# Half of one adaLN vector computed on another engine, and three changes of order, in a two-layer diffusion trunk

## The chip, the cores and the metric

The kernel runs on one core of one Trainium2 chip. The metric is the device time of one execution in microseconds. Five engines work side by side, each on its own in-order queue: PE (TensorE) multiplies matrices, DVE (VectorE) and ACT (ScalarE) work elementwise, POOL (GpSimd) does very little here, and SP (SyncE) issues nearly all DMAs.

## The reference, cut to what matters

All arrays are float32: 256 latent tokens and 256 context tokens of width 2048, two layers. Layer 0 mixes tokens with a bidirectional RG-LRU block, layer 1 with a multi-scale pooling mixer; each is followed by a SwiGLU feed-forward network (FFN) of hidden width 5632. Every sub-layer is wrapped by adaLN and a DeepNorm post-norm:

```
m = split(silu(c) @ mod_w[i] + mod_b[i], 6)           # six vectors of 2048 per layer
h = x * (1 + m[1]) + m[0]
x = LN(ALPHA * x + m[2] * mixer(h)) * ln_g[i,0] + ln_b[i,0]
h = x * (1 + m[4]) + m[3]
x = LN(ALPHA * x + m[5] * ((silu(h @ w1) * (h @ w3)) @ w2)) * ln_g[i,1] + ln_b[i,1]
```

Each adaLN vector is a product of one row of 2048 with a 2048 x 2048 matrix of 16 MB. The change concerns `m[4]` of layer 0, written (0, 4) below: the scale of the first FFN's input.

## The kernel before, in words

**Products.** A float32 product is made of three TensorE products: each operand is cut into a high part (`hi`, a rounded copy, by ACT, line 205) and a low part (`lo`, the rest, by DVE, line 206). `mm3` (lines 229 to 232) issues hi x hi, lo x hi and hi x lo into one PSUM bank. So each 512 KB tile of weights (`raw`, four buffers) costs one DMA, one ACT copy, one DVE subtraction and 12 to 24 matmuls.

**Stages.** The head computes the first adaLN columns (`mu_job`, eight loads of two 256 KB pieces for chunk 0) and the first 256 channels of the modulated input (`xc_job` loads context and latents, `fin_a` and `fin_b` modulate them). The front (24 to 177 us) does the other chunks and part of the RG-LRU input projection of pairs 0 to 4. The pair loop (177 to about 655 us) goes over 8 pairs of RG-LRU blocks: input projection (`wx_job`: 3 jobs in each of pairs 0 to 4, 8 in each of pairs 5 to 7, since `SPLIT` is 5), convolution, gate projection (8 `gate_job`), block gates and the recurrence, whose elementwise work runs on DVE and ACT. Then come the output projection, FFN 0, the pooling mixer with its four groups (about 1560 to 1615 us), FFN 1 and the last normalization.

**adaLN vectors in the loop.** Besides its own work the loop computes three adaLN vectors in two ways. `mod_chunk` works on PE: for 512 columns it loads eight pieces of 512 KB, multiplies them with the conditioning vector (`cm`, line 367, four products side by side in four strips of 32 rows), copies the bank out (`keep_part`) and turns the row into columns with four small matmuls (line 387). Vector (0, 4) is made of four such chunks. `mod_jobs` works on DVE: for 1024 columns it loads sixteen 512 KB tiles (`mraw`, two buffers) and adds each, times one conditioning scalar, to an accumulator (`acc`, two buffers; line 267, the first of the sixteen on line 264 or 261). `sums` then adds over the partitions with two matmuls per 512 columns (lines 302 and 303), and `finish_cols` copies the row to DRAM and reads it back as columns (lines 308 to 320). Vectors (0, 3) and (0, 2) go this way, 64 tiles in all; (0, 2) has no `sums` there, since `row_now` (line 335) makes it after the loop.

**Order.** A list of jobs `J` is written out by hand; `spread_mod` lays a lane of jobs (the adaLN work) among the jobs of the loop by a density per job. `Runner` goes through the list: loads are issued ahead as far as the buffers of their class allow, the hi/lo cuts up to three weight jobs ahead of the products. A job that is a `barrier` holds back the cuts of all later jobs until it has been reached. At build time a planner then fixes each engine's queue: among the instructions that are ready by its own estimates it takes the earliest in this order, and inside `tc.high_priority(HP)` an instruction counts as 400 places earlier. So work whose data are ready can move far ahead of its place.

**The pool's end.** For each pool group g, `pool_job(g, 1)` first restores the affine of the earlier norm on its 512 columns (`restore`: times `rowg`, plus `rowb`, lines 863 and 864, for two halves of the tokens), then finishes the products, adds them to the residual (`residual`, lines 836, 839 and 842, the last being the statistics) and, for g = 3, makes the moments (lines 852 to 854). `pool_end` reloads `rowg` and `rowb` by DMA; then FFN 1 begins with `hidden_t` (lines 949 to 969): normalize, transpose on PE, modulate and cut. `hidden_t`, and `residual` for g = 3, run at high priority.

Of the kernel before, what the change touches and what calls it, by code (L numbers as in the profile page):

```python
# [10 lines left out]
F32 = mybir.dt.float32  # L11
F32R = mybir.dt.float32r
AF = mybir.ActivationFunctionType
ALU = mybir.AluOpType
# [4 lines left out]
KT = D // 128  # L19
# [3 lines left out]
PAIRS = 8  # L23
PW = 352
SPLIT = 5
ROWS = (128, 128, 96)
WINDOWS = (2, 4, 8, 16)
ALPHA = 4.0 ** 0.25
# [4 lines left out]
HP = 400  # L33
# [124 lines left out]
def trunk(es, tc, x, ctxlat, cols_in, ccols, mod_w, mod_b, ln_g, ln_b, ffn_w1, ffn_w3, ffn_w2,  # L158
# [34 lines left out]
    def plain(fn):  # L193
        j = Job()
        j.use = lambda _: fn()
        return j
# [111 lines left out]
    def finish_cols(layer, which, n, bank):  # L308
# [5 lines left out]
        if n == D // MW - 1:  # L314
# [4 lines left out]
            b = cols[:, C_MODB + (layer * 6 + which) * KT:C_MODB + (layer * 6 + which + 1) * KT]  # L319
            nc.vector.tensor_tensor(t, m, b, op=ALU.add)  # L320

    def finish_row(layer, which, n, bank, width=MW):
        c = st["row", layer, which][:, n * width:(n + 1) * width]
        nc.vector.tensor_tensor(c, bank, c, op=ALU.add)
        if (n + 1) * width == D and layer == 1 and which == 2:
            pool_rows()
# [15 lines left out]
    def mod_chunk(layer, which, n):  # L342
        js = []
        ready = []
        out = {}

        def piece(q):
            j = Job()
            j.cls = "mp"

            def load():
                raw = P.tile([128, 1024], F32, name="jit", bufs=3)
                nc.sync.dma_start(raw.rearrange("p (a f) -> p a f", a=2),
                                  mod_w[layer, q * 256:(q + 1) * 256,
                                        which * D + n * 512:which * D + (n + 1) * 512]
                                  .rearrange("(a p) f -> p a f", p=128))
                return raw

            def use(j):
                ready.append((q, j.raw))  # L360
                if q % 2 == 0:
                    return
                for r, raw in ready:
                    for a in range(2):
                        kk = 2 * r + a
                        g = kk % 4
                        nc.tensor.matmul(bk[MBANK][32 * g:32 * g + 32, :], cm[:, kk, :],
                                         raw[:, a * 512:(a + 1) * 512], start=kk < 4, stop=kk >= 12)
                ready.clear()
                R.free("mp")  # L370
                R.free("mp")
                if q == 7:
                    keep_part()

            j.load = load
            j.use = use
            return j

        def keep_part():
            out[0] = P.tile([128, 512], F32, name="mh")  # L380
            nc.scalar.copy(out[0], bk[MBANK])

        def columns():
            m = out[0]
            b = bk[MBANK]
            for a in range(4):
                nc.tensor.matmul(b[:, 2 * a:2 * a + 2], m[:, a * 128:(a + 1) * 128], selt, start=True, stop=True)
            if n == 0:
                mcols[layer, which] = P.tile([128, KT], F32, name=f"mc{layer}{which}")
            o = C_MODB + (layer * 6 + which) * KT + 4 * n  # L390
            nc.vector.tensor_tensor(mcols[layer, which][:, 4 * n:4 * n + 4],
                                    b[:, 0:8].rearrange("p (a s) -> p a s", s=2)[:, :, 0],
                                    cols[:, o:o + 4], op=ALU.add)

        js = [piece(q) for q in range(8)]
        js.append(None)
        js.append(plain(columns))
        return js

# [60 lines left out]
    def xc_job(u):  # L460
        j = Job()
        j.cls = "xc"

        def load():
            xc = S_pool.tile([128, 2, 512], F32, name="xc", bufs=2)
            nc.sync.dma_start(xc, ctxlat[u * 256:(u + 1) * 256, :].rearrange("(a p) t -> p a t", p=128))
            chunks[u] = xc
            v = xc[:, :, 256:].rearrange("p a (r c) -> p a r c", r=4)
            if u < 4:
                e = per[:, 2 * u:2 * u + 2].unsqueeze(3).broadcast_to((128, 2, 4, 64))  # L470
            else:
                e = pec[:, 2 * u - 8:2 * u - 6].unsqueeze(2).broadcast_to((128, 2, 4, 64))
            nc.gpsimd.tensor_tensor(v, v, e, op=ALU.add)

        j.load = load
        j.use = lambda _: None
        return j
# [90 lines left out]
    def head():  # L568
        for q in range(8):
            J.append(mu_job(0, q))  # L570
            if q == 5:
                J.append(xc_job(0))
        J.append(plain(lambda: (fin_a(0), fin_b(0))))

    head()
# [137 lines left out]
    def recur(p, d):  # L713
# [50 lines left out]
        for f in (f2, f3, f4, f5):  # L764
# [3 lines left out]
    VF = [(0, 5, finish_row), (1, 1, finish_cols), (1, 0, finish_cols),  # L768
          (1, 3, finish_cols), (1, 4, finish_cols), (1, 2, finish_row)]
    loop = []  # L770
    for p in range(PAIRS):
        k0 = 10 if p < SPLIT else 0
        for kt in range(k0, KT, 2):
            loop.append(wx_job(p, kt, 0, kt == k0, kt == KT - 2))
        if p:
            loop.extend(gates(p - 1, 1))
        loop.append(plain(lambda p=p: conv(p)))
        for kt in range(0, KT, 2):
            loop.append(gate_job(p, kt))
        loop.extend(gates(p, 0))  # L780
    ml = []
    for n in range(4):
        ml += mod_chunk(0, 4, n)
    loop = spread_mod(loop, ml, [(len(loop), 1)])
    mv = mod_jobs([(0, 3, finish_cols), (0, 2, None)])
    loop = spread_mod(loop, mv, [(len(loop), 1)])


    def open_rows():
# [409 lines left out]
    def pool_job(g, q):  # L1199
        def use(j):  # L1200
            hi, lo = j.hl

            def token(tok):
                for a in range(2):
                    kt = 4 * g + 2 * q + a
                    ts = slice(tok * 128, (tok + 1) * 128)
                    mm3(bk[4 + (2 * g + tok) % 4], st["ph"][:, kt, ts], st["pl"][:, kt, ts],
                        hi[:, a * 512:(a + 1) * 512], lo[:, a * 512:(a + 1) * 512],
                        q == 0 and a == 0, q == 1 and a == 1)

            held.append(token)
            if q == 0 and g < PH:
                held.pop()
                token(0)
                token(1)
            if q == 1:
                for tok in range(2):
                    restore(g, tok)
                for tok in range(2):
                    for h in held:  # L1220
                        h(tok)
                    with tc.high_priority(HP if g == 3 else 0):
                        residual(bk[4 + (2 * g + tok) % 4], tok, g, st["row", 1, 2], 1.0)
                        if g == 3:
                            moments(tok)
                held.clear()
        return wjob(two_kt(pool_w[0, g], q * 256, 0, 512), 128, 1024, use)
# [11 lines left out]
    def pool_end():  # L1239
        load_ln_rows(1, 0)  # L1240
    J.append(plain(pool_end))

    f1 = ffn(1, True)
    m5 = mod_jobs([(1, 5, finish_row)])
# [106 lines left out]
```

## Time and profile before

| | us |
|---|---|
| median of three runs (2390.62 to 2395.70) | 2395.68 |
| the profiled execution | 2388.36 |
| its span | 2386.6 |
| PE busy | 2324.9 (97%) |
| DVE busy | 1758.9 (74%) |
| ACT busy | 1232.2 (52%) |
| PE idle at the pool's end, in one piece | 8.71 |

The span runs from the first to the last instruction of the profile; the execution's own time is 1.8 us longer. Busy times are unions, so a PE that is always busy may still issue more or fewer matmuls per microsecond. The granted clock of PE is full (2.4 GHz) save for a few short stretches, of which one lies at the pool's end.

### The profile page before, as it was taken

Reading aid. Unit: us, or ns where it says so; the run is one execution under the profiler, and the core shown is the slowest. Engines: PE = TensorE matmul, PEld = TensorE weight load, DVE = VectorE, ACT = ScalarE, POOL = GpSimd, SP = SyncE. Lnnn points to the kernel's source line nnn. Section 1 sums busy time; section 2 is a strip of 40 time slices with the busy share of each in tenths; the row PEclk is TensorE's granted clock in tenths of the full one; section 3 lists DMA queues with packets and bytes.
Section 4 is the critical chain, followed back from the end, with each engine's and each line's share of the span. In section 5 each row is a group of like instructions: output and inputs, shape, how many; then the busy total and the mean of one; then the engine's idle time right before and its main releaser. Section 6 shows DMA issues by size and latency. Waiting matters only on the chain. (4 is left out here: it accounts for less than half of the span.)

```text
span 2386.6 us, 29002 instructions
## 1 busy us (share of the span) xinstructions
PE 2324.9 (97%) x10488; PEld 1833.9 (77%) x10488; DVE 1758.9 (74%) x2114; ACT 1232.2 (52%) x1577; POOL 10.3 (0%) x14
## 2 busy tenths in 40 slices
PE   8999999999999999999999999998999999999997
PEld 4557777777777788877787878776878888888886
DVE  2658999887689998887887878689774544555655
ACT  3216888667685544444444455574444444444453
POOL 0000000000000000000000000000000000000000
PEclk9999999999999999999999999998999999999999
DMA  9877766776468799999999898655886656655554
GB/s 322 275 257 266 221 217 213 234 233 211 138 224 320 265 328 327 365 328 347 353 338 329 281 319 275 202 172 199 313 304 190 193 185 188 190 187 186 188 189 135
DMA packets 289704, 597.15 MB, mean 250 GB/s; under 512 B 31236, under 2 KB 99844, under 8 KB 287512
## 3 DMA queue, kind: packets, MB, share of 16 engines
q1 hardware_dynamic: 289560, 595.30, 73.9%
q8 instruction: 82, 1.34, 0.2%
q14 instruction: 62, 0.51, 0.1%
HBM read 590.20 MB, written 2.14 MB: 248 GB/s over the span
## 5 line engine op out<-in xcount | busy, mean ns | idle before, releaser
L205 ACT CAST hi<-raw 128x1024 fp32r<-128x1024 f32 (+2 forms) x740 | 733.7, 997 | 819.6 <-PE bank L231 665.9
L206 DVE TENSOR_TENSOR lo<-raw,hi 128x1024 fp32r<-128x1024 f32 (+2 forms) x740 | 849.9, 1154 | 408.8 <-ACT hi L205 390.6
L231 PE MATMUL bank<-hi,hl 128*128 128x512 f32 x1696 | 663.5, 391 | 0.0
L230 PE MATMUL bank<-hi,hh 128*128 128x512 f32 x1440 | 564.9, 393 | 0.4 <-ACT hi L205 0.3
L232 PE MATMUL bank<-lo,hh 128*128 128x512 f32 x1440 | 555.0, 392 | 5.6 <-DVE lo L206 5.0
L231 PEld LDWEIGHTS bank<-hi,hl 128*128 128x128 f32 x1696 | 319.0, 188 | 67.0 <-DVE hl L1195 0.4
L232 PE MATMUL bank<-lo,jit 128*128 128x512 f32 x880 | 347.1, 395 | 1.5 <-DVE lo L206 1.5
L230 PE MATMUL bank<-hi,jit 128*128 128x512 f32 x880 | 347.9, 396 | 0.3 <-ACT hi L205 0.3
L232 PEld LDWEIGHTS bank<-lo,hh 128*128 128x128 f32 x1440 | 270.7, 188 | 71.7 <-DVE lo L206 15.6
L230 PEld LDWEIGHTS bank<-hi,hh 128*128 128x128 f32 x1440 | 271.2, 189 | 56.7 <-ACT hi L205 1.6
L267 DVE SCALAR_TENSOR_TENSOR acc<-mraw,tiny,acc 128x1024 f32<-128x1024 f32 x172 | 220.2, 1280 | 58.2 <-DMA mraw<-in_mod_w 57.3
L232 PEld LDWEIGHTS bank<-lo,jit 128*128 128x128 f32 x880 | 165.4, 188 | 42.8 <-DVE lo L206 4.3
L230 PEld LDWEIGHTS bank<-hi,jit 128*128 128x128 f32 x880 | 165.4, 188 | 41.7 <-ACT hi L205 0.7
L231 PE MATMUL bank<-hTh,lo 128*128 128x512 f32 (+1 forms) x384 | 153.1, 400 | 0.0
L232 PE MATMUL bank<-hTl,hi 128*128 128x512 f32 (+1 forms) x384 | 151.7, 396 | 0.0
L230 PE MATMUL bank<-hTh,hi 128*128 128x512 f32 (+1 forms) x384 | 149.4, 404 | 1.8 <-ACT hTh L533 1.8
L231 PE MATMUL bank<-hi,jit 128*128 128x512 f32 x368 | 145.7, 396 | 2.6 <-DVE jit L873 2.6
L267 DVE SCALAR_TENSOR_TENSOR acc<-jit,tiny,acc 128x1024 f32<-128x1024 f32 x98 | 125.3, 1280 | 20.9 <-DMA jit<-in_mod_w 20.2
L231 PE MATMUL bank<-hi,hh 128*128 128x512 f32 x256 | 101.7, 397 | 0.0
L230 PEld LDWEIGHTS bank<-hTh,hi 128*128 128x128 f32 (+1 forms) x384 | 67.8, 179 | 40.5 <-ACT hi L205 8.4
L231 PEld LDWEIGHTS bank<-hTh,lo 128*128 128x128 f32 (+1 forms) x384 | 69.3, 181 | 28.6 <-DVE u L566 4.2
L231 PE MATMUL bank<-xh,lo 128*128 128x512 f32 (+3 forms) x224 | 89.5, 400 | 0.0
(161 smaller groups left out, 2392.2 us busy)
## 6 DMA issues: line engine op xcount, KB each, us to landing
raw<-in_ffn_w SPq DMA_DIRECT2D x528, 512.0 KB
mraw<-in_mod_w SPq DMA_DIRECT2D x184, 512.0 KB
jit<-in_mod_w SPq DMA_DIRECT2D x136, 512.0 KB
mu<-in_mod_w SPq DMA_DIRECT2D x128, 256.0 KB
raw<-in_rg_w_x SPq DMA_DIRECT2D x64, 352.0 KB
raw<-in_rg_w_gate SPq DMA_DIRECT2D x64, 352.0 KB
raw<-in_rg_w_out SPq DMA_DIRECT2D x44, 512.0 KB
raw<-in_rg_wri SPq DMA_DIRECT2D x32, 416.0 KB
```

The source lines that it names most:

```text
L205: nc.scalar.copy(hi[:k, :n], raw[:k, :n])
L206: nc.vector.tensor_tensor(lo[:k, :n], raw[:k, :n], hi[:k, :n].bitcast(F32), op=ALU.subtract)
L230: nc.tensor.matmul(bank, lh, rh, start=start, stop=False)
L231: nc.tensor.matmul(bank, ll, rh, start=False, stop=False)
L232: nc.tensor.matmul(bank, lh, rl, start=False, stop=stop)
L267: nc.vector.scalar_tensor_tensor(a, raw, c, a, op0=ALU.mult, op1=ALU.add)
```

## The change

One constant and one function are new. Vector (0, 4) is now split: columns 1024 to 2047 stay on PE (chunks 2 and 3), columns 0 to 1023 join the DVE lane, between (0, 3) and (0, 2), with the new `finish_half`. The lane's density is 0.45 over pairs 0 to 4 and 1 over pairs 5 to 7, where it was even. Counted from the lists, the lane had 34 tiles in pairs 0 to 4 and 30 in pairs 5 to 7; it now has 28 and 52. In the head, `xc_job(0)` goes behind all eight `mu_job`s, where it stood behind the sixth. `restore` for pool group 3 gets high priority. `pool_end` becomes a barrier.

```diff
+EARLY = 0.45
...
+    def finish_half(layer, which, n, bank):
+        if n == 0:
+            st["md"] = DR.tile([1, 1024], F32, name="mdh")
+        r = P.tile([128, MW], F32R, name="ml").bitcast(F32)[0:1]
+        nc.scalar.copy(r, bank[0:1, :])
+        nc.sync.dma_start(st["md"][:, n * MW:(n + 1) * MW], r)
+        if n == 1:
+            m = P.tile([128, KT], F32, name="mcr")
+            nc.sync.dma_start(m[:, :8], st["md"].rearrange("o (k p) -> p (o k)", p=128))
+            if (layer, which) not in mcols:
+                mcols[layer, which] = P.tile([128, KT], F32, name=f"mc{layer}{which}")
+            o = C_MODB + (layer * 6 + which) * KT
+            nc.vector.tensor_tensor(mcols[layer, which][:, :8], m[:, :8], cols[:, o:o + 8], op=ALU.add)
...
-            if n == 0:
+            if (layer, which) not in mcols:
                 mcols[layer, which] = P.tile([128, KT], F32, name=f"mc{layer}{which}")
...
     def head():
         for q in range(8):
             J.append(mu_job(0, q))
-            if q == 5:
-                J.append(xc_job(0))
+        J.append(xc_job(0))
         J.append(plain(lambda: (fin_a(0), fin_b(0))))
...
         for kt in range(k0, KT, 2):
             loop.append(wx_job(p, kt, 0, kt == k0, kt == KT - 2))
+            if kt == k0:
+                heads.append(loop[-1])
...
-    for n in range(4):
+    for n in (2, 3):
         ml += mod_chunk(0, 4, n)
     loop = spread_mod(loop, ml, [(len(loop), 1)])
-    mv = mod_jobs([(0, 3, finish_cols), (0, 2, None)])
-    loop = spread_mod(loop, mv, [(len(loop), 1)])
+    mv = mod_jobs([(0, 3, finish_cols), (0, 4, finish_half, 0), (0, 2, None)])
+    early = loop.index(heads[SPLIT])
+    loop = spread_mod(loop, mv, [(early, EARLY), (len(loop) - early, 1)])
...
                 for tok in range(2):
-                    restore(g, tok)
+                    with tc.high_priority(HP if g == 3 else 0):
+                        restore(g, tok)
...
     J.append(plain(pool_end))
+    J[-1].barrier = True
```

## Rows read from the trace of the kernel before

**Rows 1.** The page's first part: busy us, share of span, instructions.

```profile
PE 2324.9 (97%) x10488; PEld 1833.9 (77%) x10488; DVE 1758.9 (74%) x2114; ACT 1232.2 (52%) x1577; POOL 10.3 (0%) x14
```

**Rows 2.** Windows: stretch, length; busy PE, PEld, DVE, ACT, POOL (counts); clock, DMA, GB/s.

```profile
24.00:176.90 152.90, 152.90 (x723) 90.54 (x723) 84.09 (x165) 40.21 (x63) 7.53 (x6) 0.99 0.87 284
176.90:432.50 255.60, 253.12 (x1262) 200.86 (x1259) 237.72 (x343) 204.18 (x295) 0.00 (x0) 1.00 0.69 224
432.50:655.00 222.50, 218.05 (x1053) 170.83 (x1050) 169.55 (x231) 148.43 (x209) 0.00 (x0) 1.00 0.65 208
1632.30:2368.00 735.70, 734.47 (x3257) 601.85 (x3256) 426.79 (x416) 336.52 (x380) 0.00 (x0) 1.00 0.64 206
```

**Rows 3.** Timeline of PE around one group of `mod_chunk`, and its small matmuls.

```profile
197.93 0.32 PE L232 MATMUL bank<-lo,hTh 128*128 128x352 f32 x1
198.18 1.06 PE L367 MATMUL bank<-jit,cm 128*32 128x512 f32 x8
199.18 0.43 PE L230 MATMUL bank<-hi,hTh 128*128 128x352 f32 x1
...
294.69 0.95 PE L387 MATMUL bank<-selt,mh 128*128 128x2 f32 x8
```

**Rows 4.** Lines by form: count, busy us, mean ns, idle before.

```profile
L367 PE MATMUL bank<-jit,cm 128*32 128x512 f32 x128 | 23.9, 604 | 0.0
L302 PE MATMUL bank<-mh,onesr 128*128 128x512 f32 x32 | 12.7, 396 | 0.0
```

**Rows 5.** Tile `mraw` in 180:430 and 430:620; ns min/median/max, first and last start.

```profile
L267 DVE SCALAR_TENSOR_TENSOR acc<-mraw,tiny,acc x32: 1268/1279/1287, 182.8 to 403.4; 128x1024 f32<-128x1024 f32 x32
L267 DVE SCALAR_TENSOR_TENSOR acc<-mraw,tiny,acc x28: 1271/1284/1286, 433.0 to 552.7; 128x1024 f32<-128x1024 f32 x28
```

**Rows 6.** Timeline of PE where `row_now` reads the lane's last accumulator.

```profile
728.08 1.89 PE L335 MATMUL bank<-acc,onesr 128*128 128x512 f32 x4
```

**Rows 7.** Waits in the loop: PE 157:640, DVE 430:620 (total us, times, longest).

```profile
PE bank L232 <- DVE lo L206: 2.6, 5, 1.0
DVE acc L267 <- DMA mraw<-in_mod_w: 19.0, 13, 2.4
```

**Rows 8.** Timeline of the head: SP's issues, then what the first product waits for.

```profile
2.59 6.68 SPq L488 DMA_DIRECT2D mu<-in_mod_w  x12
9.60 0.37 SPq L466 DMA_DIRECT2D xc<-in_ctxlat  x1
16.24 1.04 POOL L473 TENSOR_TENSOR xc<-xc,per 128x512 f32<-128x512 f32 x1 [14.94 <-DMA xc<-in_ctxlat]
19.30 1.05 PE L501 MATMUL bank<-mu,cm 128*32 128x512 f32 x4 [0.45 <-DMA mu<-in_mod_w]
22.38 1.38 DVE L532 TENSOR_SCALAR xc<-xc,mc 128x256 f32<-128x256 f32 x4
23.87 1.17 PE L230 MATMUL bank<-hTh,hi 128*128 128x512 f32 x3 [1.79 <-ACT hTh L533]
```

**Rows 9.** Timeline of DVE, then PE, at the pool's end.

```profile
1612.05 1.22 DVE L206 TENSOR_TENSOR lo<-raw,hi 128x1024 fp32r<-128x1024 f32 x1
1616.40 0.68 DVE L836 TENSOR_TENSOR z<-bank,rowm 128x512 f32<-128x512 f32 x1
1617.60 1.27 DVE L863 TENSOR_TENSOR xt<-xt,rowg 128x512 f32<-128x512 f32 x2
1618.80 1.28 DVE L864 TENSOR_TENSOR xt<-xt,rowb 128x512 f32<-128x512 f32 x2
1622.56 1.16 DVE L206 TENSOR_TENSOR lo<-raw,hi 128x1024 fp32r<-128x1024 f32 x1
1623.87 0.50 DVE L859 TENSOR_SCALAR xt<-xt,mv 128x512 f32<-128x512 f32 x1
...
1624.42 2.12 PE L956 MATMUL bank<-ident,xt 128*128 128x128 f32 x8 [8.71 <-DVE xt L859]
```

**Rows 10.** Window over the end of PE's idle stretch, columns as in rows 2.

```profile
1624.40:1632.00 7.60, 6.88 (x23) 5.11 (x24) 7.09 (x18) 4.14 (x10) 0.00 (x0) 0.50 0.40 146
```

More of the change, by code (lines that the diff above doesn't have):

```diff
@@ L770, in trunk @@
     loop = []
+    heads = []
     for p in range(PAIRS):
```

## The prediction

> **What bounds the kernel now.** I read the engine line first: PE is busy for 97% of the span, DVE for 74%, ACT for 52% [rows 1]. A busy PE need not be a bound PE, so the windows by stage come next, and in them the number of matmuls per microsecond. In FFN 1 nothing but PE is loaded (DVE 427 of 736 us, DMA 0.64), and PE issues 3257 matmuls in 735.7 us, one per 0.226 us. In the pair loop, where DVE is busy for 93% (237.7 of 255.6 us) in pairs 0 to 4 and for 76% (169.6 of 222.5 us) in pairs 5 to 7, the products keep the same pace [rows 2]: matmuls of 352 columns follow each other at 0.16 us, and what breaks the stream is a group of `mod_chunk` products, not a wait [rows 3]. The waits say so too: over the whole loop PE waits 2.6 us, in five pieces, for `lo` [rows 7]. So the loop is bound by the amount of PE work, with DVE close behind in its first part and with 53 us of idle DVE in its second.
>
> A rule of the Trainium skill would read this otherwise. "Perfetto Trace Analysis", section "Identifying the Most-Contended Engine", holds matmul busy time a bad measure, since matmuls are pipelined, and asks for the busy share of the weight loads, here 77%; by that PE would have room, and taking work from it would bring less than its length. The equal pace in stages of unequal DVE load speaks against room; what it would make of the time stands with the rivals.
>
> Two places are bound otherwise. In the head PE waits for the first chunk's weights, and then for one chain through ACT and DVE [rows 8]. At the pool's end PE stands for 8.71 us in one piece, until DVE has normalized the first columns [rows 9], and then runs for some microseconds at 1.2 GHz, a granted clock of 0.50 [rows 10].
>
> **The change part by part.**
>
> *PE work in the loop.* Two of four chunks go. A group of eight passes holds PE from 198.18 to 199.18; with the slower matmul before and behind it, it costs about 1.2 us where 0.16 would pass [rows 3]. The 128 passes cover 23.9 us [rows 4], which is more than 16 groups of one microsecond, since some groups are cut in two by late pieces. Half of it is 12.0 us. The small matmuls cost 0.95 us per chunk [rows 3], so 1.9 us go for two. Added are two `sums`, four full matmuls that follow each other at 0.226 us: 0.9 us. Net 13.0 us less on PE. From both sides: with no group cut, 8 x 1.0 + 1.9 - 0.9 = 9 us; with 1.2 us for each of the ten or so pieces and a stall or two going with them, 16 us. I take 13.0.
>
> *DVE work in the loop.* Added are 16 tiles at 1.28 us [rows 5], 20.5 us, and two `lo` cuts of `sums` and a column add, some 1.5 us. The small DMAs of `finish_half` and the two row copies on ACT have no one waiting for them: the scale is needed only by FFN 0 at 797 us. What decides is where the tiles fall. The lists give 34 and 30 tiles before, 28 and 52 after. Pairs 0 to 4 thus lose six tiles, 7.7 us of DVE time, in the part where DVE is fullest, which costs nothing and may help. Pairs 5 to 7 gain 22, 28 us. DVE's idle time there is 222.5 - 169.6 = 52.9 us [rows 2], of which 19.0 us are waits for a tile's DMA [rows 7], 0.7 us per tile. If each new tile waits as long, the need is 28 + 1.5 + 15 = 45 us: it fits, but narrowly within the 53 us that are there with the waits included. Beyond them the lane has more room: its last tile is now added at 552.7 [rows 5], while the accumulator is read at 728.08 [rows 6]. 52 tiles from 433 on may take (728 - 433) / 52 = 5.7 us each; now they come every (552.7 - 433.0) / 28 = 4.3 us [rows 5], which ends the lane at 655.
>
> A tile is an in-order DVE instruction: behind one that waits for its DMA stand `lo` cuts and the recurrence. The longest such wait is 2.4 us and PE's from `lo` is 1.0 us at most [rows 7], as the cuts run two or three weight jobs ahead, about 4 us of PE each. SP's queue gets more tiles too, each waiting for a buffer that DVE frees, with `raw` loads behind them; PE shows no wait for `raw` in the loop. Nothing in the trace shows this lane at 52 tiles, so I bound the toll from both sides: a gain of 2 us, if lighter pairs 0 to 4 lose their small waits, and a loss of 8 us, if PE's waits grow in pairs 5 to 7 as DVE's share goes from 76% to (169.6 + 29.7) / 222.5 = 90%. Pairs 0 to 4 run at 93% with few waits, and are the nearest case, so I take a loss of 1.5 us. The loop nets 13.0 - 1.5 = 11.5 us.
>
> *The head.* `xc` is 512 KB and is issued at 9.60, ahead of the last four pieces of weights, whose product is at 19.30 [rows 8]. At 293 to 322 GB/s (the page's first slice is 322) those bytes take 1.6 to 1.8 us, so the last weights can come about 1.6 us sooner, and with them the chain from 19.30 to the modulation at 22.38 and the first product at 23.87. `xc` itself comes later, by the last two jobs' 1 MB, 3.3 us: the POOL add would go from 16.24 to about 19.5 and end at 20.6, just before the modulation at 22.38 - 1.6 = 20.8. It fits with nothing to spare; if `xc` is later by 2 us, the gain is gone and slightly reversed. The front behind it is dense on PE (152.9 of 152.9 us [rows 2]), so what is won stays won. I take 1.2 us, between -0.5 and 1.7.
>
> *The pool's end.* Behind the last product of group 3, DVE does the scaling at 1616.40, then four restores from 1617.60 to 1620.00, the residual, the statistics and the moments; between them stand three `lo` cuts for FFN 1, of which rows 9 show the first and the last (1612.05 and 1622.56). DVE has no gap there. High priority takes the restores, 2.4 us, out of the stretch behind the product, because their data are ready long before; the barrier puts the three cuts, 3.4 us, behind the moments. Since DVE was full before the product too, the restores only change places: what shortens the way to the normalization at 1623.87 is the 3.4 us of cuts, less what DVE now waits. Against it: PE's first product of FFN 1 needs one `hi` and one `lo`, so 1.1 us comes back into the stretch behind the transposes, and the restores may push the cuts of group 3's own operand, on which the product waits. Bounds: a gain of 5 us, if PE's stand shrinks so far that its clock stays up for the products that now run at 0.50 [rows 10], and a loss of 3.4 us, if all three cuts stand between PE and FFN 1 and the restores' gain is eaten by a later product. I take 2.0 us. The barrier holds back only cuts; loads still run as far as four `raw` buffers allow, and the loads of `rowg` and `rowb`, which wait for the restores, come earlier on SP.
>
> *Sum.* 11.5 + 1.2 + 2.0 = 14.7 us off the profiled execution's 2388.4, which gives 2373.7. The median of the runs shown lies 7.3 us above that execution, so the time to compare is 2395.7 - 14.7 = 2381.
>
> **The rivals.**
>
> *The ends win nothing.* In the pool the planner puts the restores among group 3's cuts and the three FFN cuts all stand before PE's first product: 3.4 us lost; the head gives 0. With the loop as forecast: 2395.7 - 11.5 + 3.4 = 2388. For it: DVE without a gap in that stretch. Against: the work that must precede the normalization is less by the cuts. Chance 0.14.
>
> *DVE takes over in pairs 5 to 7.* The toll is 8 us and a little more as `sums` and the recurrence are late; the loop wins 13 - 10 = 3, the ends 1: 2392, within the noise. For it: 19 us of waits at 28 tiles, and 90% or more at 52. Against: pairs 0 to 4 at 93%. Chance 0.11.
>
> *PE had room.* Then the groups taken out were filled gaps, and the loop gives nothing: 2395.7 - 3.2 + 1.5 = 2394. For it: weight loads at 77% [rows 1]. Against: 0.226 us per matmul everywhere [rows 2]. This is what the skill's rule named above would make of it; the trace does not agree. Chance 0.04.
>
> *Slower: the lane misses its reader.* If a tile in pairs 5 to 7 takes as long as now in pairs 0 to 4, (403.4 - 182.8) / 31 = 7.1 us [rows 5], only 295 / 7.1 = 41 of 52 are done when PE reaches `row_now` at 728. PE then stands for 11 tiles at about 2 us each (1.28 and 0.7 of DMA), 22 us: 2395.7 - 14.7 + 22 = 2403. It decides from 5.7 us per tile on. For it: the recurrence of three pairs has precedence. Against: 4.3 us per tile now, in these pairs. Chance 0.05.
>
> **How the numbers follow.** The forecast has the remaining 0.66; its own range is 2374 to 2388, from the loop's 9 to 16 us less the toll, and the ends. The likeliest time is 2381. The range of 2371 to 2394 takes in the two rivals near no change and, below, the head and the pool at their best; outside lie the slower rival and some of the scatter of runs, which spread over 5 us. About 0.2%, 4.8 us, is what a measurement of this kernel can tell from no change. Faster by more means under 2390.9: nearly all of the forecast (0.64), most of the first rival (0.11), a third of the second (0.04) and little of the third (0.01), together 0.80. Slower by more than 0.2% has the slower rival and a rest, 0.06. Within 0.2% there remains 0.14.
>
> **What would show each step right or wrong.** On PE, 64 passes of line 367 in place of 128, covering about 12 us, and four more matmuls of lines 302 and 303. On DVE, 80 tiles in the loop, the last between 630 and 700 us, and waits for them of 30 to 40 us; a PE wait for `lo` in the loop of more than 8 us speaks for the second rival, a PE wait at line 335 for the slower one, a loop as long as before with fewer passes for the third. In the head the first product at 22 to 23 us. At the pool's end the restores of group 3 before the last product, no FFN cut before the moments, and PE's stand under 7 us; if it stays at 8 us or the product itself is later by 2 us, that step is wrong. The forecast as a whole fails if the time is not under 2391.

## The result, and the profile after

The changed kernel takes 2380.8 us (median of four runs, 2378.5 to 2384.7), the kernel before 2394.3 us (four runs, 2390.6 to 2395.7). The ratio is 0.9945, interval 0.9931 to 0.9959: 13.2 us less, between 9.8 and 16.5. The forecast was 2381.0, a gain of 14.7 us on a base of 2395.7. The total hit; which of its terms did is another matter, and most of what follows is about that.

The first part of the page after, to be read beside [rows 1]: PE has 76 instructions and 14 us less, DVE 20 us more, and the shares hardly move.

```profile
PE 2310.8 (97%) x10412; PEld 1836.3 (77%) x10412; DVE 1778.6 (75%) x2131; ACT 1236.6 (52%) x1581; POOL 10.9 (0%) x14
```

The windows of the same stages, columns as in [rows 2]: the front from the first product to pair 0, pairs 0 to 4, pairs 5 to 7, FFN 1.

```profile
25.00:171.30 146.30, 146.30 (x723) 92.55 (x723) 83.26 (x165) 40.36 (x62) 8.00 (x6) 0.98 0.88 288
171.30:427.40 256.10, 247.64 (x1217) 200.47 (x1214) 235.48 (x338) 202.54 (x292) 0.00 (x0) 0.99 0.66 209
427.40:652.60 225.20, 220.29 (x1039) 175.11 (x1038) 195.59 (x263) 156.91 (x221) 0.00 (x0) 0.99 0.72 230
1625.80:2361.20 735.40, 734.13 (x3263) 602.25 (x3262) 429.28 (x422) 340.27 (x389) 0.00 (x0) 1.00 0.63 207
```

Two things stand against the prediction's picture. The front, where only 1.2 us at its start was to be won, is 146.3 us long in place of 152.9. And the loop, which was to give 11.5 us, is as long as before (256.1 and 225.2 us for 255.6 and 222.5), though PE issues 59 instructions less in it: PE's busy time fell in pairs 0 to 4 from 253.1 to 247.6 us, and its idle time there grew from 2.5 to 8.5.

The passes of the chunks did go, as [rows 4] had them at 128, and the lane has grown: 75 added tiles in the two stretches for 60 in [rows 5], the last at 620.8.

```profile
L382 PE MATMUL bank<-jit,cm 128*32 128x512 f32 x64 | 14.3, 603 | 0.0
...
L268 DVE SCALAR_TENSOR_TENSOR acc<-mraw,tiny,acc x32: 1270/1280/1287, 176.3 to 425.3; 128x1024 f32<-128x1024 f32 x32
...
L268 DVE SCALAR_TENSOR_TENSOR acc<-mraw,tiny,acc x43: 1272/1283/1287, 428.8 to 620.8; 128x1024 f32<-128x1024 f32 x43
```

With the first tiles of each vector, which are another form, pairs 0 to 4 have 35 tiles, as many as before, where the prediction counted 28 for 34 from the lists. The waits of PE in that stretch (total, times, longest), first before, then after:

```profile
PE bank L232 <- DVE lo L206: 1.0, 1, 1.0
```
```profile
PE bank L233 <- DVE lo L207: 5.1, 8, 1.1
PE bank L688 <- ACT gtok L676: 1.9, 1, 1.9
```

One profiled execution doesn't settle some microseconds here: the profiled ones of before and after have spans 6.9 us apart (2386.6 and 2379.7) where the timed runs differ by 13.2, and a second one of the kernel before had 2392.0. So each term is weighed below by several traces and by timed runs. This is how long the stages are in all of them (us, between the starts of named products in each trace: first product; pair 0's first input product; first output-projection product; first transpose of FFN 0; first product of the pool; first transpose of FFN 1; end).

```
                          to first  front   loop   output  FFN 0   pool   rest
                          product                  proj.
before                      23.87  152.98  482.40  140.10  771.80  53.27  762.15
before, second profile      24.28  154.18  482.63  140.12  774.79  54.00  761.97
e1_loop_only                25.60  153.15  475.61  141.80  774.71  53.28  762.40
e2_head_only                25.01  145.11  485.83  140.51  773.04  53.27  763.50
e3_pool_only                25.43  153.25  484.69  141.99  775.58  50.37  763.60
e5_last_piece_first         27.34  144.44  482.96  140.68  774.96  53.26  764.70
e8a_restore_only            23.61  152.73  483.47  140.80  777.33  50.38  765.26
e8b_barrier_only            24.05  152.92  481.95  139.53  770.82  49.95  765.96
after                       25.00  146.28  481.34  141.81  773.08  50.39  761.76
e7_thin_tiles               24.57  145.82  478.81  140.47  774.17  50.38  763.55
e10_thin_first_vector       24.57  144.77  473.71  141.53  777.75  51.20  761.65
e11_after_last_piece        24.07  147.27  483.21  140.81  771.95  50.37  760.80
e12_even_lane               24.85  145.70  484.59  141.08  776.03  50.36  760.59
e13_last_piece_later_lane   24.18  146.74  476.48  150.37  776.39  50.42  762.27
```

The boundary between loop and output projection moves with the order of the work (in the last row about 25 products changed sides), so front, loop and output projection are also summed: 774.4 to 779.9 us, mean 776.7, in the five traces in which neither front nor loop is changed; 769.4 after. FFN 0 varies by 7 us, and much of the scatter between executions is there.

### The profile page after: what moved, and what is told of

The parts are those of the page before. It is cut to its first block, busy times and chain, and to the rows that moved or that the text cites. A ratio compares the mean times of both kernels' runs of the same rounds, so it can differ in the third digit from the quotient of the medians.

```text
span 2379.7 us, 28901 instructions
## 1 busy us (share of the span) xinstructions
PE 2310.8 (97%) x10412; PEld 1836.3 (77%) x10412; DVE 1778.6 (75%) x2131; ACT 1236.6 (52%) x1581; POOL 10.9 (0%) x14
## 5 line engine op out<-in xcount | busy, mean ns | idle before, releaser
L268 DVE SCALAR_TENSOR_TENSOR acc<-mraw,tiny,acc 128x1024 f32<-128x1024 f32 x187 | 239.5, 1281 | 71.7 <-DMA mraw<-in_mod_w 70.8
L233 PE MATMUL bank<-xl,hi 128*128 128x512 f32 (+3 forms) x224 | 89.2, 398 | 0.0
```

Source lines behind the costliest of these rows:

```text
L233: nc.tensor.matmul(bank, lh, rl, start=False, stop=stop)
L268: nc.vector.scalar_tensor_tensor(a, raw, c, a, op0=ALU.mult, op1=ALU.add)
```

## The experiments

**The three parts by themselves.** `e1_loop_only` is the change without the head's and the pool's edits.

> The kernel before with the half vector moved to VectorE and the uneven lane; head and pool end as before. Forecast's step: 11.5 us faster than before (13.0 us less work on TensorE, 1.5 us of new waits). Rival from the trace of the changed kernel (waits for lo, sums and row_now give the work back): within 2 us of before. By the planner's queue the first 24 runs of mu products stay as before (28 groups cut small), so the stretch from the first product to pair 0 should keep its 153 us under both; in the loop the line-of-chunk products go from 21 groups to 11.

Measured: ratio 0.9992 (0.9981 to 1.0003), 1.9 us less, not told from nothing. That is the mark of the rival; the forecast's 11.5 us are excluded. The one trace is kinder to the loop: 475.6 us, the shortest but one of those above, and 770.6 for the sum of the three stages. In pairs 0 to 4 it has 32 tiles, since the planner placed them otherwise, and yet PE waits for `lo` there as in the kernel after:

```profile
PE bank L233 <- DVE lo L207: 5.2, 8, 1.0
```

`e2_head_only`:

```diff
         for q in range(8):
             J.append(mu_job(0, q))
-            if q == 5:
-                J.append(xc_job(0))
+        J.append(xc_job(0))
```

> The kernel before with only xc_job(0) behind all eight mu jobs. Forecast's step: 1.2 us faster, all of it before the first product of the front. Rival (the new order leads the planner to put the mu products of the front into 19 groups in place of 29, while the first product comes 1 us later): 5 to 7 us faster, all of it between the first product and pair 0, and the first product at about 25.0 us in place of 23.9.

Measured: 0.9982 (0.9972 to 0.9992), 4.3 us less. The first product comes no sooner (25.01), but the front behind it is 145.1 us in place of 153, so the whole of the kernel's shorter front comes from the place of one load in a list, and not from what this place was forecast to bring. What in the front is shorter is its chunk products on line 501 (the `mu` pieces), here windows of that line alone over the front, of before, then of this kernel: the length, PE busy and passes, weight loads, clock, DMA, GB/s.

```profile
24.00:176.90 152.90, 37.50 (x224) 6.34 (x224) 0.99 0.87 284
```
```profile
25.00:170.10 145.10, 31.21 (x224) 6.23 (x224) 0.99 0.90 297
```

It is the same 224 passes in 6.3 us less. They stand in fewer groups: 29 before, 19 here. The timeline of PE shows it, from 33 to 60 us, of before and then of the kernel after, which has the same head:

```profile
33.99 1.92 PE L501 MATMUL bank<-mu,cm 128*32 128x512 f32 x16
...
40.24 1.90 PE L501 MATMUL bank<-mu,cm 128*32 128x512 f32 x10
...
46.47 1.06 PE L501 MATMUL bank<-mu,cm 128*32 128x512 f32 x6
...
52.73 1.91 PE L501 MATMUL bank<-mu,cm 128*32 128x512 f32 x12
...
55.46 1.05 PE L501 MATMUL bank<-mu,cm 128*32 128x512 f32 x4
```
```profile
36.42 1.92 PE L516 MATMUL bank<-mu,cm 128*32 128x512 f32 x16
...
46.84 1.92 PE L516 MATMUL bank<-mu,cm 128*32 128x512 f32 x16
...
53.92 1.90 PE L516 MATMUL bank<-mu,cm 128*32 128x512 f32 x10
```

Sixteen passes take PE 1.9 us, ten take 1.9 us, and six or four take 1.05: it is nearly the number of groups that is paid for. Counted with the slower products before and behind each group, the 224 passes cost 41.7 us in 29 groups and 34.0 in 19, so 0.77 us for a group more. The code writes one burst for the pieces that have landed; with `xc` off its place in the list, the planner's order lets more of them come together.

`e3_pool_only`:

> The kernel before with only the restores of pool group 3 at high priority and the barrier at the pool's end. Forecast's step: 2.0 us faster, the stand of TensorE before the first transpose of FFN 1 under 7 us. Rival (the cuts come back behind the transposes): TensorE's stand is shorter but the first FFN products wait, within 1 us of before.

Measured: 0.9988 (0.9977 to 0.9999), 2.9 us less. PE's stand before the transposes is 5.8 us in place of 8.71 [rows 9]. To see what is left of that further on, the way is also counted to a mark about 60 us into FFN 1, its first transpose of hidden values (line 995), the 229th matmul of FFN 1 in every trace when the transposes of its input are left out. From the pool's first product to this mark the trace has 111.9 us; five traces without the edit have 112.4 to 114.0, mean 113.1.

`e4_before_again` is the kernel before, timed as if it were another.

> The kernel before itself, for a second profile. If the profiled execution of before was an ordinary one, the stages take the same times to about 1 us and the span is 2386.6 us give or take 2. If it was a lucky one, the span is some 6 us longer, and the difference sits in stages that the change does not touch, or in the loop, where the gain that the first profiles don't show would then lie.

Measured: 1.0000 (0.9990 to 1.0009). So about 2.3 us is what twelve runs tell apart, and the loop's 1.9 alone is under it.

The three parts give 1.9 + 4.3 + 2.9 = 9.1 us by themselves, 13.2 (9.8 to 16.5) together. Each has some 2.5 us of uncertainty, so whether they add up or help each other stays open. The traces can be grouped by edit as well. Up to pair 0, six traces with the old head take 176.3 to 178.8 us, mean 177.7, and five with the new one 169.3 to 171.3, mean 170.3 (the turned bursts below left out): 7.3 us less. Loop and output projection take 621.5 to 626.7 us, mean 623.9, in the seven traces without the loop's edits, and 617.4, 623.2 and 624.0 in the three that have them as in the changed kernel (alone, after, and `e11_after_last_piece` below): 2.4 us less. The pool's end, up to the mark in FFN 1, has 1.6 less (below). By this count the head is more than half of the gain, and the loop a small part of it.

**Does the number of groups make the front's gain?** `e5_last_piece_first` leaves the head's order as before and writes each burst from its last piece to its first, which lets PE's first pass wait for the latest of the loads and then run through.

```diff
-            for r, raw in burst:
+            n = 0
+            for r, raw in reversed(burst):
...
-                                     raw[:, a].rearrange("p m f -> p (m f)"), start=kk < 4, stop=kk >= 12)
+                                     raw[:, a].rearrange("p m f -> p (m f)"),
+                                     start=q < 4 and n < 4 and burst[0][0] == 0,
+                                     stop=q == 7 and n >= 2 * len(burst) - 4)
+                    n += 1
```

> The kernel before, the mu products of a burst issued from the last loaded piece to the first, so that the burst cannot begin before its last piece is there; nothing else moves, xc_job(0) stays behind the sixth job. If the front's gain is a matter of how many groups the mu products are cut into (29 before, 17 here by the planner's queue, 0.77 us per group by the traces), the stretch from the first product to pair 0 falls from 153 us to 144 or 146 and the time by 4 to 8 us. If the gain came from the earlier weights or another effect of the head's order, the stretch stays at 153 us and the time within 1.5 us of before.

Measured: 0.9973 (0.9961 to 0.9985), 6.5 us less than before. The front is 144.4 us, in 17 groups that cost 32.6 us, though the first product comes 3.5 us later than before (27.34). Another edit with the same effect on the groups has the same effect on the front; it isn't the load's place as such. `e11_after_last_piece` has the same edit on the kernel after, for `mu` pieces and for chunks:

```diff
-                for r, raw in ready:
+                for r, raw in reversed(ready):
```

> The changed kernel with the bursts of mu products and of the vector's chunks issued from the last loaded piece to the first. By the planner's queue the mu products come in 17 groups in place of 19 and the chunk's in 12 as before, so by the price of 0.77 us per group 1.5 us less in the front, and a time within 3 us of the changed kernel. If the order of the front matters beyond the groups (the head was 3 us later in the run with this edit alone), it is slower than the changed kernel by up to 2 us.

Measured: 0.9947 (0.9934 to 0.9961), against 0.9945 of the kernel after. The 1.5 us in the front did not come: it is 147.3 us long and reaches pair 0 at 171.3, as after. PE is busy there for 2 us less (144.3 us, for 146.3), but now stands for 3.0 us, until ACT has cut the weights:

```profile
PE bank L231 <- ACT hi L206: 3.0, 2, 1.6
```

**Where the loop's gain went: DVE in which pairs?** The second rival had it in pairs 5 to 7, where the tiles were added. `e7_thin_tiles` is the kernel after in which fifteen of the sixteen new tiles add only 32 of 1024 columns (the rest of that vector's sum is left out); loads and waits stay.

```diff
+                        if (layer, which) == (0, 4) and kt > 0:
+                            a = acc[0][:, :32]
+                            nc.vector.scalar_tensor_tensor(a, raw[:, :32], c, a, op0=ALU.mult, op1=ALU.add)
+                            return
```

> The changed kernel, but VectorE adds only 32 of 1024 columns of fifteen of the sixteen new tiles (the loads stay, so 992 columns of the vector's half are left out): TensorE's relief without some 18 us of VectorE's new load. If the loop gave its gain back because VectorE is late (waits for lo, sums and row_now), the stretch from pair 0 to the output projection is 4 to 8 us shorter than in the changed kernel and the time too. If the relief was never worth 13 us, or the tiles' DMAs are what delays, it stays within 1.5 us of the changed kernel.

Measured: 0.9937 (0.9919 to 0.9955), against 0.9945 (0.9931 to 0.9959): no difference that can be told, with about 16 us less on DVE; the loop is 2.5 us shorter in the trace, between the two marks. PE's idle time in pairs 5 to 7 is 3.8 us here, 4.9 after and 4.5 before, so by these traces the new tiles' DVE time costs PE about 1 us there; the timed runs alone would leave room for more. `e10_thin_first_vector` does the same to 30 tiles of (0, 3), which all run in pairs 0 to 4 (the edit with `(0, 3)` in place of `(0, 4)`, so that this vector's sum is what is left out).

> The changed kernel, but VectorE adds only 32 of 1024 columns of thirty of the 32 tiles of vector (0, 3), which lie in pairs 0 to 4 (992 of 1024 columns of both halves are left out; the loads stay). If VectorE bounds pairs 0 to 4, as the waits for lo there say (5.7 us in all, and the same 256 us as before in spite of 7 us less TensorE work), the stretch from pair 0 to pair 5 falls from 256 us to 248 or less and the time by 4 to 8 us against the changed kernel. If it is TensorE's queue or the loads that bound it, the stretch stays within 2 us of 256.

Measured: 0.9928 (0.9913 to 0.9943): by the ratios 4 us less than the kernel after, which the intervals don't tell from nothing. By the trace it is clear: front, loop and output projection take 760.0 us, 9.4 less than after and 5 less than in `e7_thin_tiles`. The window of pairs 0 to 4, and PE's wait in it:

```profile
169.30:415.10 245.80, 243.20 (x1217) 199.28 (x1214) 205.05 (x339) 204.39 (x295) 0.00 (x0) 1.00 0.67 214
```
```profile
PE bank L233 <- DVE lo L207: 0.5, 1, 0.5
```

PE has the same 1217 products there as after and does them in 10.3 us less; DVE is busy for 83% of the time in place of 92%, and the eight waits for `lo` are one. Of the 10.3 us, 5.9 are idle time of PE; the other 4.4 are a shorter busy time, in which the granted clock (1.00 for 0.99) has a part. So in the kernel after DVE holds PE back in pairs 0 to 4.

**Was the uneven density worth something?** `e12_even_lane` is the kernel after with the lane spread evenly:

```diff
-EARLY = 0.45
+EARLY = 1.0
```

> The changed kernel with EARLY at 1, an even lane: by the planner's queue 44 tiles in place of 35 ahead of the 100th cut, that is in pairs 0 to 4. If VectorE bounds these pairs, nine tiles at 1.28 us lengthen the stretch from pair 0 to pair 5 by 8 to 12 us and the time by 6 to 12 us against the changed kernel. If it does not, the time stays within 2 us of the changed kernel.

Measured: 0.9962 (0.9949 to 0.9975), 4 us slower than after by the ratios, with the loop 3.3 us longer and 41 tiles in pairs 0 to 4 for 35; the intervals overlap. The 8 to 12 us expected in pairs 0 to 4 and the 6 to 12 in the time did not come; the stretch is some 3 us longer (see the table below). `e13_last_piece_later_lane` goes the other way, `EARLY = 0.1` on `e11_after_last_piece`.

> The run with both bursts turned, and EARLY at 0.1: by the planner's queue 31 tiles ahead of the 100th cut in place of 35, and the last at the same place. If VectorE bounds pairs 0 to 4, four tiles less shorten them by up to 5 us against the run with both bursts turned; if not, the time stays within 1.5 us of it.

Measured: 0.9970 (0.9960 to 0.9981), against 0.9947 (0.9934 to 0.9961) with 0.45: 5.5 us slower, though the intervals still touch. It is no test of four tiles, since `e11_after_last_piece` has 31 tiles there too, and one ahead of pair 0. Products of the last pairs end up behind the first output-projection product, and loop and output projection together are 626.9 us for 624.0. So 0.45 has the lowest time of the three densities, without being clear of either.

The runs with different numbers of tiles can be set side by side. The time is counted from pair 0's first product to the 1100th product of projections and gates behind it, near the end of pair 4, so that all have the same of these products, with the tiles that DVE has added by then:

```
                            us   tiles
e12_even_lane             251.3     41
after                     248.0     34
e11_after_last_piece      243.4     31
e1_loop_only              242.6     32
e13_last_piece_later_lane 241.0     30
e10_thin_first_vector     238.2     32, of which 30 thin
before                    247.7     35
```

From 41 tiles to 30 the way is 10 us shorter, some 0.9 us a tile, where a tile takes DVE 1.28 us [rows 5]. Each row is one trace; the seven without the loop's edits, at 34 or 35 tiles, have 245.8 to 250.2 us. It is DVE's work that counts and not the tiles' loads: `e10_thin_first_vector` loads as many as `e1_loop_only` and is 4.4 us sooner. So with half of the chunks gone DVE sets the pace in pairs 0 to 4, and the changed kernel, at 34 tiles, is no sooner there than the kernel before. Fewer tiles there are not the whole remedy: `e11_after_last_piece` and `e13_last_piece_later_lane` lose behind pair 4 what they have won.

**Which half of the pool's edit?** `e8a_restore_only` has the high priority alone, `e8b_barrier_only` the barrier alone, one execution each.

```diff
-                    restore(g, tok)
+                    with tc.high_priority(HP if g == 3 else 0):
+                        restore(g, tok)
```
```diff
     J.append(plain(pool_end))
+    J[-1].barrier = True
```

> The kernel before with only the restores of pool group 3 at high priority. By the prediction's reason (the restores only change places, the cuts behind the barrier are what shortens the way) the stretch from the pool's first product to the first transpose of FFN 1 stays within 0.7 us of the 53.3 to 54.0 us of before. Rival (the restores are the 2.4 us that go): it falls to 50.4 to 51.2 us, as with both edits.

> The kernel before with only the barrier at the pool's end. By the prediction's reason the stretch from the pool's first product to the first transpose of FFN 1 falls by about 3 us, to 50.4 to 51 us, as with both edits. Rival (the restores are the gain): it stays at 53.3 to 54.0 us, the place of the cuts being filled by the restores.

Measured (their single times, 2395.3 and 2387.0, say nothing of 2 us): PE at FFN 1's first transposes, of the priority alone and then of the barrier alone, with the idle time before each group in brackets.

```profile
1628.31 1.11 PE L956 MATMUL bank<-ident,xt 128*128 128x128 f32 x4 [5.80 <-DVE xt L859]
```
```profile
1619.22 1.12 PE L956 MATMUL bank<-ident,xt 128*128 128x128 f32 x4 [4.61 <-DVE xt L859]
```

Either one brings the first transpose 3 us nearer (50.4 and 50.0 us behind the pool's first product, for 53.3), so at this point the priority meets its rival's mark and the barrier that of the prediction's reason, and either half seems to do the whole. Counted to the mark in FFN 1 they part: the priority alone has 112.0 us, the barrier alone 114.5, both together 110.8 to 112.2 (seven traces, mean 111.5), neither 112.4 to 114.0 (mean 113.1). By these traces, one of each half and only some 0.5 us outside the spread, the restores' priority makes the gain, and the barrier alone gives back what it wins. The order on DVE shows how. With the priority alone the work at the pool's end stands as with both edits, save that one FFN cut runs 0.7 us earlier and one residual behind it. With the barrier alone two restores of group 3 still stand behind the last product, one of them behind the first normalization; the second half of the tokens so gets its moments 57.1 us behind the pool's first product, for 54.6 with the priority alone, and PE waits once more, at a later transpose. DVE, then PE, of the barrier alone:

```profile
1621.73 0.68 DVE L864 TENSOR_TENSOR xt<-xt,rowb 128x512 f32<-128x512 f32 x1
1626.40 0.26 DVE L852 BATCH_NORM_AGGREGATE mv<-stats 128x2 f32<-128x24 f32 x1
...
1632.27 1.09 PE L956 MATMUL bank<-ident,xt 128*128 128x128 f32 x8 [1.60 <-ACT z L962]
```

## Why the prediction was right, and where only its total was

**The total is right, at 2380.8 for 2381.0, and so is the sign of each part; but two terms were off in opposite directions, so the hit is luck.** The loop was put at 11.5 us and is worth 1.9 (timed alone) to 6.0 (beside the others), the head at 1.2 and is worth 4.3 timed and 7.3 in the traces, the pool at 2.0 and measured 2.9 timed and 1.6 in the traces.

*The loop, the over-sized term.* Its PE side came out at the lower end of the forecast. The 64 passes that are left cover 14.3 us where 12 were expected. All that breaks the stream there (the chunks' groups, the small products, `sums` and `row_now`), with what the products beside it lose, cost 35.6 us before and costs 27.2 after: 8.4 less, or 10.6 without the waits in it, where 13.0 were put and 9 to 16 were the bounds. What failed is the toll of 1.5 us, and in it the sentence that pairs 0 to 4 lose six tiles, "which costs nothing and may help". They lost none. The lists put a tile beside the n-th job, but the planner runs ahead of the list, and by the trace 35 tiles fall there before and after. So the stretch with the fullest DVE got none of the relief, and once PE had less to do there, DVE's pace showed: eight waits for `lo` for one. The products of `row_now` in the loop, whose bank the chunks also use, wait for DVE's `mc`, and those behind them for `hi`; with the small products ahead of them they cost 4.5 us beyond the pace in place of 1.8:

```profile
627.04 1.12 PE L350 MATMUL bank<-acc,onesr 128*128 128x512 f32 x2 [1.25 <-DVE mc L406]
629.05 0.66 PE L231 MATMUL bank<-hi,hTh 128*128 128x352 f32 x1 [0.89 <-ACT hi L206]
```

By time the loop's edits give 1.9 us alone (-0.7 to 4.5), and 13.2 - 4.3 - 2.9 = 6.0 us beside the other two, with about 5 us of uncertainty. Both are under 11.5.

"PE is bound by its own work, DVE close behind" was thus true before, and no longer after, in pairs 0 to 4: `e10_thin_first_vector` and the count by tiles show it. The equal pace of products in stages of unequal DVE load, on which the prediction rested, says only which engine is the bound now; it doesn't say how far the next one is behind. DVE's 93% in [rows 2] did.

*The second rival*, DVE taking over, had the right mechanism and the wrong pairs. In pairs 5 to 7 DVE fits as forecast (87% busy). Its waits for a tile's DMA over the loop are 38.5 us, within the 30 to 40 expected (23.9 of them in pairs 5 to 7), and its last tile is at 620.8, a little ahead of the 630 to 700:

```profile
DVE acc L268 <- DMA mraw<-in_mod_w: 38.5, 34, 2.6
```

PE's waits for `lo` stay under the 8 us that were to speak for this rival: 5.7 us over the loop, for 2.6 [rows 7], nearly all in pairs 0 to 4.

*The third rival*, PE with room, would also make the loop give little. The shorter loop of `e10_thin_first_vector` with all PE work kept might look like it. But FFN 1 keeps its one matmul per 0.225 us (735.4 / 3263) with its weight loads at 82%, and in `e10_thin_first_vector` pairs 0 to 4 are 99% PE. So the rule on weight loads that the prediction cited from the Trainium skill ("Perfetto Trace Analysis", "Identifying the Most-Contended Engine") doesn't find the limit here; FFN 1 and the end take 760.6 to 766.0 us in all fourteen traces.

*The slower rival* did not come about: `row_now` reads the last accumulator at 723.0, more than 100 us behind the lane's last tile for it.

*The head, right only in its sign.* The step "the last weights come 1.6 us sooner, and with them the first product" failed. The weights' product is 1.08 us sooner than in [rows 8], the first product 1.13 later:

```profile
18.22 1.05 PE L516 MATMUL bank<-mu,cm 128*32 128x512 f32 x4 [0.44 <-DMA mu<-in_mod_w]
19.58 1.04 POOL L488 TENSOR_TENSOR xc<-xc,per 128x512 f32<-128x512 f32 x1 [18.28 <-DMA xc<-in_ctxlat]
21.31 2.11 DVE L547 TENSOR_SCALAR xc<-xc,mc 128x256 f32<-128x256 f32 x4
21.78 1.16 POOL L488 TENSOR_TENSOR xc<-xc,per 128x512 f32<-128x512 f32 x1 [1.16 <-DMA xc<-in_ctxlat]
23.12 1.14 ACT L548 CAST hTh<-xc 128x512 fp32r<-128x512 f32 x2 [3.23 <-DVE xc L547]
24.17 1.45 ACT L206 CAST hi<-raw 128x704 fp32r<-128x704 f32 x2
25.00 1.22 PE L231 MATMUL bank<-hTh,hi 128*128 128x512 f32 x2 [3.99 <-ACT hi L206]
```

POOL's first add, at 19.6, came as forecast; its second, which belongs to the next chunk and which the prediction left out, falls on the modulation, which takes 2.11 us for 1.38 [rows 8]; and on ACT the weights' cast `hi`, at 20.88 before, now stands behind the casts of `xc`. With the old head the first product is at 23.6 to 24.3 in four traces and at 25.4 and 25.6 in two others, where the last weights' product ran at 1.2 GHz; with the new one it is at 24.1 to 25.0 in seven. The gain comes from the front, which the prediction took as dense and so as fixed: "dense" was right (PE busy 146.3 of 146.3 us), but PE was busy with more groups than it needed. The forecast paid for groups in the loop [rows 3, 4] and didn't count them in the front.

*The pool's end, right in size, wrong in reason.* The stand went from 8.71 to 5.81 us, under the 7 expected, so the step's own mark was met. The clock is at 1.2 GHz (0.50) behind it as before [rows 10], so the larger gain that was the upper bound didn't come. The window behind the stand, then DVE and PE around it:

```profile
1617.00:1625.00 8.00, 5.10 (x15) 3.58 (x16) 8.00 (x18) 0.91 (x2) 0.00 (x0) 0.50 0.41 125
```
```profile
1612.42 0.68 DVE L854 TENSOR_TENSOR z<-bank,rowm 128x512 f32<-128x512 f32 x1
1615.41 0.24 DVE L870 BATCH_NORM_AGGREGATE mv<-stats 128x2 f32<-128x24 f32 x1
1616.18 1.20 DVE L207 TENSOR_TENSOR lo<-raw,hi 128x1024 fp32r<-128x1024 f32 x1
1617.30 1.91 DVE L877 TENSOR_SCALAR xt<-xt,mv 128x512 f32<-128x512 f32 x4
...
1617.90 1.11 PE L974 MATMUL bank<-ident,xt 128*128 128x128 f32 x4 [5.81 <-DVE xt L877]
```

One FFN cut still stands between the moments and the normalization, as before, and the restores are gone from behind the scaling. The prediction held that the restores "only change places" and the 3.4 us of cuts shorten the way. But of the three cuts only the last and the end of the second stood behind the last product, which ends at 1615.7 in [rows 9]; and the restores found room ahead of that product, which starts 44.2 us behind the pool's first in the traces of before, of after and of the priority alone. The two halves, each in one trace, show 1.1 us won by the restores alone and 1.4 lost by the barrier alone.

Still open: why the loop's edits are worth 1.9 us alone and some 6 beside the others (or whether they are, at these intervals: by the traces loop and output projection are 6.5 us shorter alone and under 1 beside the others), what loses time behind pair 4 in the runs with few tiles ahead of it, and by which of its rules the planner groups the `mu` pieces anew when `xc` moves.

## What to carry to other kernels

Before work is taken off the busiest engine, see in each stage how full the next one is, by the windows, and count where the work handed over really falls in a trace and not in the list that a planner reads. Where a stream of products is cut by small groups, count the groups, since a group costs nearly the same with four passes as with eight. And a total that hits is not a proof of its terms: the parts have to be timed by themselves.

## What the runs showed of the hardware that was not expected

A group of chunk products (32 columns of weights, 512 of data) costs PE about 0.77 us more for each group into which the same 224 passes are cut (29 groups 41.7 us, 19 groups 34.0, 17 groups 32.6). The price goes in steps. Behind the start of a group in which no wait falls, PE issues its next other product after 0.98 to 1.00 us with two to eight passes (all but three of 352 such groups in fourteen traces), and after 1.83 to 1.86 us with ten to sixteen (all 167).

One of the four modulations on DVE (128x256) took 1133 ns, the others 402 to 411, when a POOL add on the next chunk's tile had begun 0.2 us before it; in the kernel before, where the add is all but over when they begin, all four take 407 to 414 (ns minimum, median and maximum, after and then before):

```profile
L547 DVE TENSOR_SCALAR xc<-xc,mc x4: 402/408/1133, 21.3 to 23.0; 128x256 f32<-128x256 f32 x4
```
```profile
L532 DVE TENSOR_SCALAR xc<-xc,mc x4: 407/408/414, 22.4 to 23.4; 128x256 f32<-128x256 f32 x4
```

It is 1130 to 1134 ns in each of the five traces in which the add falls so, and none of the four is over 414 in the nine others. The add itself took 1.16 us for 1.04. The Trainium skill ("SBUF — State Buffer", section "Who interferes with whom") says that VectorE and GpSimd share a pair of ports under an exclusive lock, that a `tensor_scalar` can be among the operations that need it, and that the later instruction waits for the whole of the earlier. The long modulation ends at 23.1, 0.15 us behind the add, which agrees in that it lasts until the add is over; 0.15 us is less than the 0.4 us that a modulation takes by itself. No run here moved the add alone.
